# An explicit plan of pieces for both attentions of a two-layer hybrid model

## Chip, cores and metric

The kernel runs on one core of a Trainium2 chip, in one launch. The metric is the time of an execution on the device, in microseconds (us), as the median of several runs. Engines are named as in the profile: PE is TensorE's matmul, PEld its weight load, DVE is VectorE, ACT is ScalarE, POOL is GpSimd, SP is the engine that issues most of the DMAs.

## What is computed

One sequence of 512 tokens of width 1024 passes two layers in fp32. Layer 0 mixes two kinds of attention with 8 heads each, layer 1 has one kind with 16 heads; each is followed by a feed-forward network (FFN) with a short convolution. Cut to what matters here:

```python
# layer 0, first half: heads with a cumulated forget gate c
s = q_i @ k.T * scale + c_i - c_k            # causal
out = softmax(s) @ v
# layer 0, second half: an index picks 128 keys a query
score = sum_h iw * relu(iq_h @ ik.T)         # causal, 4 index heads
sel = top_k(score, 128)
logits = (q_lat @ c_kv[sel] + q_rope @ k_rope[sel]) * scale
out = softmax(logits) @ c_kv[sel]            # then w_uv
# layer 1: blocks of 256 keys, own block and chosen earlier ones (all of them at this length)
out = softmax(concat(s_sel, s_own)) @ v
x = x + out @ w_out;  x = x + ffn(rmsnorm(x))
```

## The kernel before

Activations lie transposed, 1024 features as 8 tiles of 128 x 512. Every fp32 product is made of three matmuls of high and low parts (`mm3`, L159 to L161), so each operand is split: ACT casts the high part, DVE or POOL subtracts the low part. Weights come in chunks of 128 x 1024 (512 KB): SP loads one into a `raw` tile (three of them, L147), ACT casts it (L148), and POOL (L152, in layer 0's attention) or DVE (L154, in layer 1) makes the low part.

An attention has eight pairs of heads. The pieces of a pair are these:

- `ks`, `qs`: a projection of 24 matmuls into one of three PSUM banks named `mm`; then a scaling or a rotary embedding; then `stack_k` or `stack_q`, which put high and low parts of a head one above the other. That takes six DMAs for a k and three for a q, issued by SP (`move`, L244): for a q, two fill `a`, and a third rewrites `l` once `a` has its copy.
- `vals`, every second pair: a `v_group` of 96 matmuls of 256 columns from two weight chunks. The pairs 4 to 7 of layer 0 make k and v from a latent tile in short products instead (`mm_dk` at L705 and on, `mm_dv`).
- `soft`, for a head: four blocks of scores (L268, L269; in the first half a decay term at L344 before them), each followed by a DVE instruction that adds the mask and takes the maximum (L348) and by an exponential on ACT (L349); POOL divides (L353). The result lies in one of two `prt` tiles.
- `mix`, for a head: ten transposes (L372), their split into high and low parts (L128, L129), and eight value matmuls into one bank `o` (L381, L382).

Layer 0 also has three index scores (`index_scores`, with ReLUs at L618 and, for blocks 2 and 3, a copy on ACT and an addition on POOL at L623), and a selection for each of three blocks of queries (`select`): 16 rounds of a maximum (L629) and a replacement (L630) on DVE. They must be done before the scores of pair 4. Four parts of the output projection of pairs 0 to 3 (`out_proj("oe0_")`, `out_proj("oo0_")`) need only those pairs.

The order of the text comes from `heads`. A work list holds the pieces with the pair that they are due for; before a pair all work due for it is emptied, after each softmax a share of the work due for the next pair is done, and the value products run one head behind:

```python
            for e in range(2):
                probs = soft(...)
                n = len([1 for w in work if w[0] <= p + 1])
                for _ in range((n + 1 - e) // (2 - e)):
                    work.pop(0)[1]()
                if prev is not None:
                    finish(prev)
                prev = (p, e, probs)
```

Written in the letters of the change (s a softmax, m a value product, k, q, v the projections, i an index score, x a selection, o a part of the output projection; the first digit is the pair), the old order of layer 0 is: v0 i1 k0 i2 q0 i3, s00 k1 s01 q1 m00, s10 v2 k2 m01 s11 q2 x1 m10, s20 k3 x2 (first half) m11 s21 q3 x2 (rest) m20, s30 k4 x3 (first half) q4 m21 s31 v4 x3 (rest) m30, s40 k5 m31 s41 q5 m40, s50 k6 q6 m41 s51 v6 m50, s60 k7 q7 m51 s61 o0 m60, s70 o1 o2 m61 s71 o3 m70, m71. Layer 1 has the same without i and x: v0 k0 q0, s00 k1 s01 q1 m00, s10 v2 k2 m01 s11 q2 m10, and so on. Its first v group holds the norm's scale in its middle (`moba_scale`: `rstd_main` and `rope_scaled`, L217).

The framework that builds the kernel does not keep this order on each engine: it places an instruction when it expects its inputs and buffers to be ready, and the text's order decides between those that are.

## Time and profile before

| | |
|---|---|
| median of 3 runs | 1262.97 us (1261.54 to 1265.60) |
| the profiled execution | 1261.51 us, of which the span of instructions 1259.7 us |
| busy in the span | PE 1220.4, PEld 1018.3, DVE 810.9, ACT 557.4, POOL 357.7 us |
| first attention | 57.4 (first index score) to 276.0 us (first FFN matmul) |
| second attention | 637.0 (first v group) to 886.0 us |
| mean granted clock of TensorE | 0.993 |

The page gives shares of the whole span. How TensorE stands in a stage is read from the stretches, and what it waits for from the waits: a row there names the instruction that waited, what released it, the total, the times and the longest. The end of a matmul is modelled in the profile, so a stretch that is full of matmuls counts as busy even where they follow each other a little more slowly.

### The profile page before, as it was taken

To read this page: it belongs to the slowest core of one execution; us is meant where nothing else is said; L and a number is where in the kernel's file an instruction comes from. 1 tells how busy PE (TensorE), PEld (TensorE's weight loads), DVE (VectorE), ACT (ScalarE), POOL (GpSimd) and SP (SyncE) were. 2 spreads that over 40 slices of the span, in tenths; PEclk is the share of its full clock that TensorE was granted. 3 is DMA by queue.
4 is the path that set the end of the run, shared out by engine and by line. 5 is a ranking of instruction groups with operands and counts; after the bars stand their busy time and mean duration, and the time that the engine had idled before them with its cause. 6 is when DMAs were issued, how large, how long until landed. Compare 5 with 4: busy or idle time off the path is not lost.

```text
span 1259.7 us, 16807 instructions
## 1 busy us (share of the span) xinstructions
PE 1220.4 (97%) x5996; PEld 1018.3 (81%) x5996; DVE 810.9 (64%) x1489; ACT 557.4 (44%) x969; POOL 357.7 (28%) x394
## 2 busy tenths in 40 slices
PE   6889999999999999999999999999999999999997
PEld 4768778778888888888887888888888888888887
DVE  7889988675654555544666778787655555444555
ACT  5564667653332333333445556555433333332334
POOL 3665557542111111111213223332222111111110
PEclk9989999999999999999999999999999999999999
DMA  5333444222333322323325434331233332333321
GB/s 194 101 92 111 128 99 128 63 80 89 101 100 100 98 90 93 96 93 100 103 96 142 113 100 123 105 109 67 84 93 108 100 100 92 94 100 101 96 88 67
DMA packets 57379, 127.24 MB, mean 101 GB/s; under 512 B 7584, under 2 KB 21024, under 8 KB 57296
## 3 DMA queue, kind: packets, MB, share of 16 engines
q1 hardware_dynamic: 56368, 124.81, 33.2%
q10 hardware_dynamic: 864, 1.17, 0.3%
q8 instruction: 47, 0.77, 0.2%
q14 instruction: 36, 0.29, 0.1%
q0 software_dynamic: 64, 0.20, 0.0%
HBM read 104.13 MB, written 2.10 MB: 84 GB/s over the span
## 4 chain that ended last, share of the span: by engine, by line
PE 79%; DVE 10%; issue 5%; ACT 3%; DMA 2%; POOL 1%; POOLq 0%; ACTq 0%; DVEq 0%; SPq 0%
PE mm_g L160 6%; PE mm_g L161 6%; PE mm_g L159 6%; PE mm_u L161 6%; PE mm_u L159 6%; PE mm_u L160 6%; PE mm_d L161 6%; PE mm_d L160 6%; PE mm_d L159 6%; DVE tmask L630 2%; DVE m L629 1%; DMA mq_l<-mq_h 1%; PE t_m L372 1%; PE o_m L381 1%; PE mm_mk L160 1%
## 5 line engine op out<-in xcount | busy, mean ns | idle before, releaser
L434 POOL TENSOR_TENSOR cv<-cv,gs 128x512 f32<-128x512 f32 x44 | 57.1, 1298 | 546.2 <-ACT gs L433 546.2
L159 PE MATMUL mm_d<-a_h,wh_d 128*128 128x512 f32 (+1 forms) x384 | 142.8, 372 | 0.0
L160 PE MATMUL mm_d<-a_l,wh_d 128*128 128x512 f32 (+1 forms) x384 | 142.6, 371 | 0.0
L161 PE MATMUL mm_d<-a_h,wl_d 128*128 128x512 f32 (+1 forms) x384 | 142.6, 371 | 0.0
L503 DVE TENSOR_TENSOR us<-mm_u,cv 128x512 f32<-128x512 f32 x44 | 30.4, 692 | 168.1 <-PE mm_u L161 132.7
L160 PE MATMUL mm_g<-xl,wh_g 128*128 128x512 f32 x352 | 137.2, 390 | 0.4 <-DVE xl L175 0.4
L159 PE MATMUL mm_u<-xh,wh_u 128*128 128x512 f32 x352 | 137.3, 390 | 0.0
L161 PE MATMUL mm_u<-xh,wl_u 128*128 128x512 f32 x352 | 137.0, 389 | 0.0
L160 PE MATMUL mm_u<-xl,wh_u 128*128 128x512 f32 x352 | 137.0, 389 | 0.0
L161 PE MATMUL mm_g<-xh,wl_g 128*128 128x512 f32 x352 | 137.0, 389 | 0.0
L159 PE MATMUL mm_g<-xh,wh_g 128*128 128x512 f32 x352 | 137.0, 389 | 0.0
L148 ACT CAST wh_g<-raw_g 128x1024 fp32r<-128x1024 f32 x44 | 46.3, 1052 | 143.1 <-PE mm_g L160 141.6
L500 DVE TENSOR_TENSOR gs<-mm_g,RB 128x512 f32<-128x512 f32 x44 | 30.4, 691 | 118.2 <-PE mm_g L161 115.7
L128 ACT CAST wh_d<-raw_d 128x1024 fp32r<-128x1024 f32 x45 | 47.4, 1054 | 123.7 <-PE mm_u L160 103.4
L160 PEld LDWEIGHTS mm_d<-a_l,wh_d 128*128 128x128 f32 x384 | 72.3, 188 | 12.5
L159 PEld LDWEIGHTS mm_d<-a_h,wh_d 128*128 128x128 f32 x384 | 72.3, 188 | 12.5
L161 PEld LDWEIGHTS mm_d<-a_h,wl_d 128*128 128x128 f32 x384 | 72.3, 188 | 12.4
L160 PEld LDWEIGHTS mm_g<-xl,wh_g 128*128 128x128 f32 x352 | 66.1, 188 | 14.8 <-DVE xl L175 1.1
L161 PEld LDWEIGHTS mm_u<-xh,wl_u 128*128 128x128 f32 x352 | 66.1, 188 | 13.8
L159 PEld LDWEIGHTS mm_g<-xh,wh_g 128*128 128x128 f32 x352 | 66.1, 188 | 13.7
L161 PEld LDWEIGHTS mm_g<-xh,wl_g 128*128 128x128 f32 x352 | 66.1, 188 | 13.7
L160 PEld LDWEIGHTS mm_u<-xl,wh_u 128*128 128x128 f32 x352 | 66.1, 188 | 13.6
(778 smaller groups left out, 3072.4 us busy)
## 6 DMA issues: line engine op xcount, KB each, us to landing
raw_g<-in_w SPq DMA_DIRECT2D x44, 512.0 KB, 3.5
raw_u<-in_w SPq DMA_DIRECT2D x44, 512.0 KB, 3.6
raw_d<-in_w SPq DMA_DIRECT2D x41, 256.0 KB, 2.9
raw_d<-in_w SPq DMA_DIRECT2D x29, 192.0 KB, 2.6
raw_d<-in_w SPq DMA_DIRECT2D x34, 128.0 KB, 2.4
raw_oe<-in_w SPq DMA_DIRECT2D x8, 512.0 KB, 4.0
raw_mv<-in_w SPq DMA_DIRECT2D x8, 512.0 KB, 3.5
raw_mk<-in_w SPq DMA_DIRECT2D x8, 512.0 KB, 4.0
```

Of the source, the lines that this page charges most:

```text
L128: A.copy(dst_h, src)
L148: A.copy(wh, raw)
L159: PE.matmul(out, ah, bh, start=first, stop=False)
L160: PE.matmul(out, ah, bl, start=False, stop=False)
L161: PE.matmul(out, al, bh, start=False, stop=last)
L372: PE.transpose(t[:, n * P:n * P + P], probs[i][:, j * P:j * P + P], ident)
L381: PE.matmul(o[:, o0:o0 + w], vj, ph[:, c0:c0 + w], start=j == 0, stop=False)
L434: G.tensor_tensor(cv, cv, gs, op=OP.mult)
L500: V.tensor_tensor(gs, og, RB, op=OP.mult)
L503: V.tensor_tensor(us, ou, cv, op=OP.mult)
L629: V.max(m8, sc)
L630: V.match_replace(sc, m8, sc, -3e38)
```

## The change

Two strings, PLAN0 and PLAN1, list the pieces of each attention in order. `attention` runs through a plan and `attend` binds the letters to functions; `heads`, the work lists and their due numbers are gone. Each piece stands once in its plan. The selections are cut into quarters of four rounds (x10 is the first quarter for block 1). In layer 1 the scale of the norm is taken by whichever projection comes first, after its matmuls, and only once. Buffer counts stay as they were.

```diff
--- before.py
+++ after.py
@@ -47,6 +47,18 @@
 
 N_BIG, N_V, N_TMP, N_COL, N_PR, N_W = 25, 2, 7, 8, 2, 3
 N_PSUM = {"mm": 3, "S": 2, "T": 2, "O": 1}
+
+
+
+PLAN0 = (
+    "v0 i1 i2 k0 q0 i3 k1 s00 s01 q1 v2 x10 s10 m00 k2 s11 x11 m01 x12 q2 x13 x20 m10 k3 m11 k4 x21 s20 "
+    "x22 x30 s21 q3 m20 s30 x31 x32 s31 q4 x23 v4 m21 m30 k5 x33 m31 s40 s41 q5 m40 k6 s50 q6 m41 s51 v6 "
+    "k7 m50 q7 s60 o0 m51 s61 m60 s70 o1 s71 m61 m70 o2 m71 o3 "
+)
+PLAN1 = (
+    "q1 q0 k0 k3 v0 s00 k1 q2 m00 k2 s01 s10 s11 q3 s20 q4 s21 m01 v2 m10 m11 k4 s30 s31 m20 m21 v4 k5 q6 "
+    "m30 q5 s40 m31 s41 m40 k6 s50 k7 s51 m41 v6 q7 o0 s60 s61 s70 m50 m51 s71 o1 m60 m61 o2 o3 m70 m71 "
+)
 
 
 def _pieces(c, bits):
@@ -524,34 +536,24 @@
                 done(2 * p + e, Q[1])
         last(Q[1])
 
-    def heads(pairs, work):
-
-
-        work = list(work)
-        prev = None
-
-        def finish(pr):
-            p, e, probs = pr
-            c = pairs[p]
-            mix(f"{c['nm']}{e}", e, probs, values[c["v"]], c["hv"] + e, c["y"])
-            if e == 1:
-                c["out"].append(halves(c["y"], f"o_{c['nm']}", c.get("lo", V)))
-
-        for p, c in enumerate(pairs):
-            while work and work[0][0] <= p:
-                work.pop(0)[1]()
-            c["y"] = tmp(f"y_{c['nm']}")
-            for e in range(2):
-                probs = soft(f"{c['nm']}{e}", e, c["q"], c["k"], c["bias"], c["decay"][e] if "decay" in c else None)
-                n = len([1 for w in work if w[0] <= p + 1])
-                for _ in range((n + 1 - e) // (2 - e)):
-                    work.pop(0)[1]()
-                if prev is not None:
-                    finish(prev)
-                prev = (p, e, probs)
-        finish(prev)
-        for w in work:
-            w[1]()
+    def attention(pairs, plan, pieces):
+
+
+        probs = {}
+        for step in plan.split():
+            kind, n = step[0], step[1:]
+            if kind == "s":
+                c, e = pairs[int(n[0])], int(n[1])
+                if e == 0:
+                    c["y"] = tmp(f"y_{c['nm']}")
+                probs[n] = soft(f"{c['nm']}{e}", e, c["q"], c["k"], c["bias"], c["decay"][e] if "decay" in c else None)
+            elif kind == "m":
+                c, e = pairs[int(n[0])], int(n[1])
+                mix(f"{c['nm']}{e}", e, probs.pop(n), values[c["v"]], c["hv"] + e, c["y"])
+                if e == 1:
+                    c["out"].append(halves(c["y"], f"o_{c['nm']}", c.get("lo", V)))
+            else:
+                pieces[kind](int(n))
 
     values = {}
 
@@ -676,7 +678,7 @@
 
         c = {"nm": f"f{p}", "v": ("f", p // 2), "hv": 2 * (p % 2), "bias": causal, "out": fo, "lo": G,
              "decay": [(selr[:, P + h:P + h + 1], ck) for h in (2 * p, 2 * p + 1)]}
-        return c, ([vals] if p % 2 == 0 else []) + [ks, qs]
+        return c, ks, qs, vals
 
     def dsa(p):
         def vals():
@@ -707,24 +709,16 @@
             c["k"] = stack_k(o, f"dk{p}")
 
         c = {"nm": f"d{p}", "v": ("d", p // 2), "hv": 2 * (p % 2), "bias": [causal[0]] + tmask[1:], "out": do}
-        return c, [ks, qs] + ([vals] if p % 2 == 0 else [])
-
-    pairs, work = [], []
-    for n in range(8):
-        c, w = (fox if n < 4 else dsa)(n % 4)
-        pairs.append(c)
-        if n == 0:
-            w = [x for i, f in enumerate(w) for x in (f, lambda i=i: index_scores(i + 1))]
-        elif n == 2:
-            w.append(lambda: select(1, range(16)))
-        elif n > 2 and n < 5:
-            w[1:1] = [lambda n=n: select(n - 1, range(8))]
-            w.append(lambda n=n: select(n - 1, range(8, 16)))
-        work += [(n, f) for f in w]
-        if n == 7:
-            work.append((7, lambda: out_proj("oe0_", fo, part=[0])))
-    work += [(8, lambda m=m: out_proj("oe0_", fo, part=[m])) for m in range(1, 4)]
-    heads(pairs, work)
+        return c, ks, qs, vals
+
+    def attend(made, plan, **pieces):
+        for k, n in (("k", 1), ("q", 2), ("v", 3)):
+            pieces[k] = lambda p, n=n: made[p][n]()
+        attention([m[0] for m in made], plan, pieces)
+
+    attend([fox(p) for p in range(4)] + [dsa(p) for p in range(4)], PLAN0,
+           i=index_scores, x=lambda n: select(n // 10, range(n % 10 * 4, n % 10 * 4 + 4)),
+           o=lambda m: out_proj("oe0_", fo, part=[m]))
     acc = sq_acc(1)
     out_proj("oe1_", do, lambda d: prep(d, 1, acc))
     lo_on_pool = False
@@ -739,33 +733,31 @@
 
 
     def moba_scale():
-        rstd_main(accs[2], "n2")
-        rope_scaled()
+
+        if 2 in accs:
+            rstd_main(accs.pop(2), "n2")
+            rope_scaled()
 
     mo = ([], [])
 
     def moba(p):
         def vals():
-            values["m", p // 2] = v_group(f"mv{p // 2}_", moba_scale if p == 0 else None)
+            values["m", p // 2] = v_group(f"mv{p // 2}_", moba_scale)
 
         def qs():
-            c["q"] = stack_q(rope(proj(f"mq{p}"), f"mq{p}"), f"mq{p}")
+            o = proj(f"mq{p}")
+            moba_scale()
+            c["q"] = stack_q(rope(o, f"mq{p}"), f"mq{p}")
 
         def ks():
-            c["k"] = stack_k(rope(proj(f"mk{p}"), f"mk{p}"), f"mk{p}")
+            o = proj(f"mk{p}")
+            moba_scale()
+            c["k"] = stack_k(rope(o, f"mk{p}"), f"mk{p}")
 
         c = {"nm": f"m{p}", "v": ("m", p // 2), "hv": 2 * (p % 2), "bias": causal, "out": mo[p // 4]}
-        return c, ([vals] if p % 2 == 0 else []) + [ks, qs]
-
-    pairs, work = [], []
-    for n in range(8):
-        c, w = moba(n)
-        pairs.append(c)
-        work += [(n, f) for f in w]
-        if n == 7:
-            work.append((7, lambda: out_proj("oo0_", mo[0], part=[0])))
-    work += [(8, lambda m=m: out_proj("oo0_", mo[0], part=[m])) for m in range(1, 4)]
-    heads(pairs, work)
+        return c, ks, qs, vals
+
+    attend([moba(p) for p in range(8)], PLAN1, o=lambda m: out_proj("oo0_", mo[0], part=[m]))
     accs[3] = sq_acc(3)
     out_proj("oo1_", mo[1], lambda d: prep(d, 3, accs[3]))
     fin = {}
```

## Rows read from the trace of the kernel before

**Rows 1.** The page, busy time and share of the span

```profile
PE 1220.4 (97%) x5996; PEld 1018.3 (81%) x5996; DVE 810.9 (64%) x1489; ACT 557.4 (44%) x969; POOL 357.7 (28%) x394
```

**Rows 2.** Stretches: PE, PEld, DVE, ACT, POOL busy (count), PE clock, DMA, GB/s

```profile
57.40:276.00 218.60, 208.91 (x1091) 171.78 (x1090) 180.19 (x455) 134.01 (x302) 132.57 (x174) 0.98 0.36 99
637.00:886.00 249.00, 243.01 (x1388) 208.07 (x1387) 188.34 (x400) 136.09 (x296) 70.17 (x86) 1.00 0.37 105
276.00:637.00 361.00, 360.46 (x1593) 297.85 (x1592) 196.32 (x250) 125.57 (x152) 67.29 (x51) 1.00 0.32 98
```

**Rows 3.** Waits of TensorE, 57.4 to 276 us: total, times, longest

```profile
PE s_f L268 <- DMA fq_a<-fq_l: 3.3, 1, 3.3
PE ix L268 <- ACT rl L618: 2.3, 1, 2.3
PE t_f L372 <- DVE pt_f_0l L129: 1.9, 4, 1.3
PE mm_dq L159 <- DVE dv L129: 1.8, 1, 1.8
```

**Rows 4.** Waits of TensorE, 637 to 886 us

```profile
PE s_m L268 <- DMA mq_l<-mq_h: 3.3, 3, 1.3
PE s_m L268 <- DMA mq_a<-mq_l: 1.0, 1, 1.0
```

**Rows 5.** Stretches at a granted clock of 0.50: PE busy, clock, DMA, GB/s

```profile
83.90:90.70 6.80, 6.13 (x19) 0.50 0.09 22
169.20:172.60 3.40, 3.40 (x9) 0.50 0.16 18
```

**Rows 6.** Timeline of TensorE at the ends of two waits

```profile
84.57 0.58 PE L268 MATMUL s_f<-fk_h,fq_a 128*128 128x256 f32 x1 [3.29 <-DMA fq_a<-fq_l]
...
168.65 0.50 PE L159 MATMUL mm_dq<-xh,wh_dq 128*128 128x512 f32 x1 [1.77 <-DVE dv L129]
```

**Rows 7.** Timeline of the SP queue, 79 to 85 us (start, length)

```profile
79.24 0.33 SPq L147 DMA_DIRECT2D raw_fq<-in_w  x1
...
80.14 0.59 SPq L244 DMA_DIRECT2D fq_a<-fq_l  x1
84.54 0.46 SPq L244 DMA_DIRECT2D fq_l<-fq_h  x1
```

**Rows 8.** Timeline of POOL, 67 to 79 us

```profile
67.61 2.84 POOL L152 TENSOR_TENSOR wl_fq<-raw_fq,wh_fq 128x256 fp32r<-128x256 f32 x4 [4.36 <-ACT wh_fq L148]
...
71.65 1.02 POOL L623 TENSOR_TENSOR tmask<-rl,cmask 128x384 f32<-128x384 f32 x1
72.75 3.21 POOL L623 TENSOR_TENSOR tmask<-rl,tmask 128x384 f32<-128x384 f32 x3
75.92 3.29 POOL L152 TENSOR_TENSOR wl_fv<-raw_fv,wh_fv 128x256 fp32r<-128x256 f32 x4
```

**Rows 9.** DMA issues: KB each, median us to landing

```profile
fq_a<-fq_l SPq DMA_DIRECT2D x1, 128.0 KB, 4.4
fq_l<-fq_h SPq DMA_DIRECT2D x1, 128.0 KB, 2.2
...
mq_l<-mq_h SPq DMA_DIRECT2D x1, 128.0 KB, 5.2
```

**Rows 10.** Selection instructions: durations min/median/max and starts; then groups of one width

```profile
L629 DVE MAX8 m<-tmask x48: 414/561/696, 67.1 to 168.5; 128x8 f32<-128x256 f32 x16, 128x8 f32<-128x384 f32 x16, 128x8 f32<-128x512 f32 x16
...
L629 DVE MAX8 m<-tmask 128x8 f32<-128x512 f32 x16 | 11.0, 685 | 0.2
L630 DVE MATCH_REPLACE8 tmask<-m,tmask 128x512 f32<-128x512 f32 x16 | 10.8, 676 | 0.0
```

**Rows 11.** Stretches of the first attention, columns as in rows 2

```profile
57.00:97.00 40.00, 34.38 (x148) 27.48 (x148) 33.75 (x94) 25.11 (x51) 28.55 (x34) 0.91 0.35 104
97.00:177.00 80.00, 76.25 (x437) 64.36 (x437) 73.63 (x191) 42.23 (x98) 41.85 (x59) 0.98 0.40 107
```

**Rows 12.** Timeline of VectorE, the scaled cosine of the second attention

```profile
648.84 0.69 DVE L217 TENSOR_TENSOR CR<-CT,RB 128x512 f32<-128x512 f32 x1 [1.22 <-ACT RB L211]
```

## Prediction

> **What bounds the kernel now.** I read the page's engine shares first, then the stretches by stage, then TensorE's waits in the two attentions, then its clock, then the rows round the longest waits.
>
> TensorE is busy for 1220.4 us of a span of 1259.7 [rows 1]. That leaves 39 us, and the change touches only part of them. The stretches [rows 2] set both attentions (57.4 to 276.0 us and 637.0 to 886.0 us) beside the FFN between them. In the FFN TensorE idles for 361.0 - 360.5 = 0.5 us. In the first attention it idles for 218.6 - 208.9 = 9.7 us, in the second for 249.0 - 243.0 = 6.0 us. The named waits there are few: in the first attention 3.3 us for a stack move of fq_a, 2.3 us for an index ReLU, 1.9 us for a low part of the transposed probabilities and 1.8 us for dv [rows 3]; in the second four waits for moves of mq, 4.3 us together [rows 4]. The clock comes on top: in two stretches of 6.8 and 3.4 us the granted clock is 0.50, which is 1.2 of 2.4 GHz [rows 5]. The first stretch begins at 83.9 us, inside the wait for fq_a, which ends at 84.57; the second at 169.2, just after the wait for dv ended at 168.65 [rows 6]. Before both falls TensorE stood idle (3.3 and 1.8 us); after the waits for mq, 1.3 us at most, the clock stays at 1.00 [rows 2]. Half a clock costs half of its busy time: 6.1/2 = 3.1 us and 3.4/2 = 1.7 us.
>
> So all that a new order can win is idle time plus clock: 9.7 + 6.0 + 3.1 + 1.7 = 20.5 us. The program computes the same work: both plans hold every piece once (8 k, 8 q, 4 v, 16 scores, 16 value products, 4 output parts, and in the first attention 3 index scores and 12 quarters of the selections).
>
> **Why the big wait happens.** The move of fq_a is issued at 80.14 us, directly behind a weight load (raw_fq) of 79.24, on the same SP queue [rows 7]. Before that the queue stood still. The load could go out only when its raw buffer was free, that is when POOL had finished the low part of an earlier weight tile (75.92 + 3.29 = 79.21 us [rows 8]). POOL was late because the four additions of index score 2 (1.02 + 3.21 us, from 71.65) came first, although it had idled for 4.36 us before 67.61 [rows 8]. Once issued, the move shared the DMA engines with 512 KB of weights: 4.4 us to landing, where the next move, with no load before it, took 2.2 [rows 9]. The moves of mq show the same: 5.2 us for mq_l [rows 9].
>
> **The change part by part.** First: the text's order is not the engines' order. The selection of block 1 stands behind q2 in the old text, but the first selection row runs at 67.1 us [rows 10], before the first score. The build places each piece as soon as its inputs and buffers are expected ready, and the text gives precedence only. The plan therefore shifts who wins a queue; it does not move whole pieces. Two heads' score rows remain bounded by the two prt buffers, which stay: a third softmax waits for a value product's transposes, whatever the plan says.
>
> *Start of the first attention* (v0 i1 i2 k0 q0 i3 k1 s00 in place of v0 i1 k0 i2 q0 i3 s00 k1). Index score 2 takes precedence over k0. Its ReLUs, its copies and its four POOL additions, 4.2 us, can then fall into POOL's idle 4.36 us. The weight tile's low part ends some 4 us earlier (near 75 us), so do the load and the moves behind it, and fq_a lands near 80.5 instead of 84.5, before TensorE's wait begins (84.57 - 3.29 = 81.3 [rows 6]). I take the wait and its half clock as gone: 3.3 + 3.1 = **6.4 us**. Bounds: 0 (POOL does not use the gap) to 6.4. I take the upper end because the gap found, 4.36, exceeds the 3.3 us that are missing.
>
> *The index wait (2.3 us)* hangs on ACT, which casts the cumulated gate first; index scores now come even earlier, so it stays: 0 (between +2.3 and -2.3, since index 2 may double it or k0 may fill it).
>
> *Selections in quarters.* Same instructions (48 maxima and 48 replacements). A quarter of block 3 is 4 x (685 + 676) ns = 5.4 us of VectorE [rows 10]. In 97 to 177 us VectorE is busy for 73.6 of 80 us [rows 11], so any quarter that wins precedence delays something: a low part of a value product or of dv. TensorE's cover is a projection, 24 matmuls of 361.0/1593 = 0.227 us [rows 2] = 5.4 us. One quarter is just covered, two in a row are not. I leave the waits for low parts and dv and their clock (1.9 + 1.8 + 1.7 = 5.4 us) where they are: net 0, bounds -5.4 to +10.5 (three places of 1.8 + 1.7 us, the places of the third rival).
>
> *Second attention* (q1 q0 k0 k3 v0 s00 in place of v0 k0 q0 s00 k1). Projections go ahead by one to three pairs, so a q's two moves into a (4.4 us behind a load) and the one back into l (5.2) must end under later work: 9.6 us. In the old order q of a pair was the last thing before its scores, with one projection (5.4 us) or less as cover. Now two projections or a v group (96 matmuls at half width, twice 5.4 = 10.9 us) mostly lie between. I take the four waits as gone: **4.3 us**; bounds 0 to 4.3.
>
> The norm's scale moves behind the first projection. It needs the transposes and the chain on VectorE to the scaled cosine at 648.84 us [rows 12], some 12 us after the stretch begins; q1, q0 and k0 hold three banks of mm, 3 x 5.4 = 16.3 us, so k3 finds q1's bank free again. Cost 0; without that cover TensorE would wait for each us that the chain is late. The guard in the scale function adds no instruction. The extra pieces ahead of q0 and k0 put three moves and a load of q1 on SP before theirs; v0's 10.9 us and k3's 5.4 us cover them.
>
> *Ends.* Value products two heads behind and o3 before or between the last ones: none of the waits of [rows 3, 4] lies at an end (they are for f, dq and mq pieces that come earlier), so 0, bounds -1 to +3.
>
> Here the page of the profile leaves room for doubt. By rows, TensorE's idle time in the second attention is 6.0 us, of which the moves are 4.3. The Trainium skill (Perfetto Trace Analysis, Identifying the Most-Contended Engine) says that headroom is to be judged by the weight loads' busy share, not by matmul busy time; that share is 208.1/249.0 = 84% in the second attention and 297.9/361.0 = 83% in the full FFN, so by the rule nothing is left there and the sum would be 6.4 alone, 1256.6 us. I keep the rows: shorter matmuls need more weight loads per us, and the waits are there by name.
>
> **Sum.** 6.4 + 4.3 = 10.7 us. The profiled execution took 1261.5 us (span 1259.7 and 1.8 around it), 1.5 under the median of 1262.97; taken off the median, 10.7 gives **1252 us**.
>
> **Rivals.**
>
> *1. The waits only change their names (1260 to 1265, say 1263).* Loads and moves keep one queue, and the sequence of weight loads hardly changes. For it: four waits of the same kind in the second attention come at irregular places, so they are where the build's expectation of a landing was too early, and it expects the same afterwards. Then 10.7 us go and come back. Against it: longer leads. The Trainium skill (DMA: Bandwidth & Descriptors, Queues, rings and completion order) says that each DMA engine consumes a queue's descriptors in ring order; the 4.4 against 2.2 us above agree, and by that rule a move behind a load stays slow under any plan.
>
> *2. Everything yields (1243).* All idle time and both half clocks go: 1263 - 20.5. For it: each wait is short, and a plan with pieces split finely has fill for each. Against it: the index wait and the selections are bound to ACT and VectorE.
>
> *3. Selections starve TensorE (1269).* The plan puts two quarters together at three places (x13 x20 before m10, x22 x30 before s21, x31 x32 before s31), just where k4 and q3 have been used up earlier. VectorE, already 92% busy [rows 11], then delays the low parts as it delayed dv: 1.8 + 1.7 us at each, 10.5 us in all. With the second attention's 4.3 us won and the first wait not, 1263 + 10.5 - 4.3 = 1269. It decides as soon as TensorE idles for more than the 9.4 us that it idles now between 57 and 177 us (5.6 + 3.8 [rows 11]) plus the 4.3 won later. Against it: the build runs selections early wherever VectorE is free, as it does now.
>
> **Chances.** The forecast 0.48, rival 2 0.12, rival 1 0.2, rival 3 0.2. A measurement of this kernel tells 0.3% (3.8 us) from no change. Faster: 0.48 + 0.12 = 0.6; same 0.2; slower 0.2. The range goes from rival 2 with the end's 1 us, 1242, to rival 3, 1269: it takes in rival 1 and the bounds of single terms, and leaves out about 2 in 10. The likeliest case alone spans 1247 to 1258 (5.4 us more won, or the first term lost).
>
> **What would show it.** Right: no wait of scores for fq_a near 81 us, POOL's additions of index 2 before 71 us, no half clock at 84 to 91 us, no wait for a mq move of over 0.3 us, TensorE's idle time in the second attention near 2 us. Wrong: a move's wait at other scores (rival 1); VectorE over 95% busy with a new half clock between 97 and 177 us (rival 3); a wait for the norm chain at the fourth projection of the second attention.

## The result and the profile after

The changed kernel takes 1245.68 us (median of 4 runs, 1245.14 to 1246.56), the kernel before, on the same chip, 1262.74 us (4 runs, 1261.54 to 1265.60). The ratio is 0.9859 with a 95% interval of [0.9842, 0.9877]: 17 us faster, where 10.7 us were forecast. The profiled execution took 1245.54 us with a span of 1243.8, so it shows 15.9 us less span than the profile of before.

The page, busy time and share of the span [rows 1]:

```profile
PE 1211.7 (97%) x5996; PEld 1012.4 (81%) x5996; DVE 812.3 (65%) x1489; ACT 556.2 (45%) x969; POOL 357.5 (29%) x394
```

The same instructions as before on every engine. TensorE is busy for 8.7 us less and its weight loads for 5.9 less; the other engines stay within 1.4 us. The stretches by stage, with the columns of [rows 2] (first attention, second attention, the FFN between them):

```profile
56.80:268.00 211.20, 203.78 (x1090) 168.34 (x1089) 180.80 (x456) 134.22 (x302) 131.99 (x174) 1.00 0.39 103
628.70:869.50 240.80, 240.12 (x1386) 206.83 (x1386) 189.34 (x400) 134.71 (x296) 70.53 (x86) 1.00 0.39 108
268.00:628.70 360.70, 360.55 (x1593) 297.82 (x1593) 195.94 (x250) 125.60 (x152) 67.18 (x51) 1.00 0.32 98
```

Against [rows 2] the first attention is 218.6 - 211.2 = 7.4 us shorter, the second 249.0 - 240.8 = 8.2 us; the FFN stays within 0.3 us, and what lies before and behind adds up to nothing (0.6 less ahead of the first attention, 0.6 more behind the second). In the first attention TensorE's busy time falls by 5.1 us and its idle time from 9.7 to 7.4 us. The granted clock there is 1.00 throughout: both half-clock stretches of [rows 5], 3.1 + 1.7 = 4.8 us by the prediction's working, are gone, and they are nearly all of the 5.1. In the second attention idle time falls from 6.0 to 0.7 us, and busy time by 2.9.

The runs agree on the clock's part: the four of the kernel after have a mean granted clock of 0.996 to 0.997, the profile of before 0.993, and the 14 to 20 runs of the kernel before beside each experiment 0.992 to 0.994 on average. Taken as lost time, (1 - clock) x 1255 us, that is an estimate, from above, of 4 to 6 of the 17 us.

TensorE's waits in the first attention, 56.8 to 268 us [rows 3]:

```profile
PE ix L280 <- ACT rl L620: 2.6, 2, 2.3
PE o_f L393 <- ACT pt_f_0h L140: 1.5, 1, 1.5
PE t_f L384 <- DVE pt_f_0l L141: 1.2, 1, 1.2
PE s_f L356 <- DVE mx_f L360: 1.0, 2, 0.7
PE s_f L280 <- DMA fq_a<-fq_l: 0.6, 1, 0.6
```

and all that is left of them in the second, 628.7 to 869.5 us [rows 4]:

```profile
PE bc_n L216 <- DVE y_n L213: 0.3, 1, 0.3
```

The wait for fq_a went from 3.3 to 0.6 us, the one for dv is gone (1.8), the one for low parts shrank by 0.7: 5.2 us in all. New are 1.5 us for a high part of the transposed probabilities and 1.0 us for the scores' maxima; with 0.3 more for the index ReLUs these take 2.8 back, and 5.2 - 2.8 = 2.4 is about the idle time won (9.7 - 7.4 = 2.3). All four waits for mq moves are gone.

Now the SP queue and POOL round the place of the old wait for fq_a. SP, 74 to 82 us [rows 7]:

```profile
74.94 0.33 SPq L159 DMA_DIRECT2D raw_fk<-in_w  x1
...
76.58 0.55 SPq L256 DMA_DIRECT2D fq_a<-fq_h  x1
77.18 0.60 SPq L256 DMA_DIRECT2D fq_a<-fq_l  x1
78.20 0.33 SPq L159 DMA_DIRECT2D raw_fq<-in_w  x1
81.60 0.46 SPq L256 DMA_DIRECT2D fq_l<-fq_h  x1
```

POOL, 66 to 79 us [rows 8]:

```profile
66.56 1.03 POOL L625 TENSOR_TENSOR tmask<-rl,cmask 128x384 f32<-128x384 f32 x1 [3.92 <-ACT rl L624]
67.66 3.21 POOL L625 TENSOR_TENSOR tmask<-rl,tmask 128x384 f32<-128x384 f32 x3
...
72.08 2.84 POOL L164 TENSOR_TENSOR wl_fq<-raw_fq,wh_fq 128x256 fp32r<-128x256 f32 x4
74.87 3.30 POOL L164 TENSOR_TENSOR wl_fv<-raw_fv,wh_fv 128x256 fp32r<-128x256 f32 x4
```

POOL's additions of index score 2 do come first now, as forecast, but they did not fill the gap: POOL idles for 3.92 us ahead of them, because ACT hands over the weighted ReLU that they add (L624) only at 66.56. They push wl_fq from 67.61 to 72.08, and wl_fv ends at 78.17, 1.0 us earlier than before and not 4. What did change is the queue: the two moves of fq_a now stand ahead of the load of raw_fq, not behind it, and go out at 76.58 and 77.18 while that load still waits for POOL (78.20, just behind 78.17). They land no faster: the third move, which waits for them, goes out at 81.60, 4.4 us behind the second, as before (80.14 to 84.54). Another load, raw_fk, stands 2.2 us ahead of that second move. What is won is the issue, 3.0 us earlier.

### The profile page after: what moved, and what is told of

Its sections match the earlier page's. It is cut to its first block, busy times and chain, and to the rows that moved or that the text cites. A ratio compares the mean times of both kernels' runs of the same rounds, so it can differ in the third digit from the quotient of the medians.

```text
span 1243.8 us, 16808 instructions
## 1 busy us (share of the span) xinstructions
PE 1211.7 (97%) x5996; PEld 1012.4 (81%) x5996; DVE 812.3 (65%) x1489; ACT 556.2 (45%) x969; POOL 357.5 (29%) x394
## 4 chain that ended last, share of the span: by engine, by line
PE 85%; DVE 8%; issue 4%; ACT 1%; DMA 1%; POOL 0%; POOLq 0%; ACTq 0%; DVEq 0%
PE mm_g L172 6%; PE mm_g L171 6%; PE mm_g L173 6%; PE mm_u L171 6%; PE mm_u L172 6%; PE mm_u L173 6%; PE mm_d L171 6%; PE mm_d L172 6%; PE mm_d L173 6%; PE t_m L384 1%; DVE tmask L632 1%; DVE m L631 1%; PE mm_mk L171 1%; PE mm_mq L173 1%; PE mm_mk L173 1%
## 5 line engine op out<-in xcount | busy, mean ns | idle before, releaser
L172 PEld LDWEIGHTS mm_d<-a_l,wh_d 128*128 128x128 f32 x384 | 72.3, 188 | 12.4
L173 PEld LDWEIGHTS mm_g<-xh,wl_g 128*128 128x128 f32 x352 | 66.1, 188 | 13.7
L171 PEld LDWEIGHTS mm_u<-xh,wh_u 128*128 128x128 f32 x352 | 66.1, 188 | 13.6
```

Of the source, the lines that this page charges most:

```text
L171: PE.matmul(out, ah, bh, start=first, stop=False)
L172: PE.matmul(out, ah, bl, start=False, stop=False)
L173: PE.matmul(out, al, bh, start=False, stop=last)
```

## The experiments

Twelve kernels, each against the kernel before on the same chip. The stage lengths are of the profiled execution, from the first matmul of a stage to the first of the next (by that count the kernel before has 248.6 in the second attention and the one after 240.7). "fq_a" and "mq" are TensorE's waits for those moves.

| kernel | median us | ratio, 95% interval | first att. | second att. | fq_a | mq |
|---|---|---|---|---|---|---|
| before | 1262.7 | | 218.6 | 248.6 | 3.3 | 4.3 |
| after | 1245.7 | 0.9859 [0.9842, 0.9877] | 211.3 | 240.7 | 0.6 | 0 |
| e1 plan 0 only | 1256.4 | 0.9960 [0.9945, 0.9975] | 212.8 | 249.2 | 0.9 | 2.9 |
| e2 plan 1 only | 1254.0 | 0.9940 [0.9922, 0.9957] | 218.8 | 240.7 | 3.6 | 0 |
| e3 i2 ahead | 1269.7 | 1.0059 [1.0041, 1.0078] | 229.8 | 250.0 | 2.3 | 1.4 |
| e5 k1 ahead | 1270.4 | 1.0072 [1.0039, 1.0106] | 225.7 | 253.1 | 3.2 | 4.4 |
| e9 i2 and k1 ahead | 1267.7 | 1.0051 [1.0031, 1.0072] | 223.7 | 250.3 | 2.0 | 2.6 |
| e12 old start, new rest | 1258.3 | 0.9971 [0.9957, 0.9985] | 216.4 | 250.9 | 3.9 | 2.0 |
| e4 moves ahead of loads | 1257.9 | 0.9962 [0.9950, 0.9975] | 217.7 | 244.5 | 0.9 | 0.2 |
| e6 selections whole | 1246.3 | 0.9892 [0.9864, 0.9920] | 211.8 | 240.4 | 0.7 | 0 |
| e7 value products later | 1264.3 | 1.0023 [1.0004, 1.0041] | 219.7 | 252.0 | 3.6 | 2.8 |
| e8 projections earlier | 1263.8 | 1.0014 [0.9996, 1.0032] | 216.7 | 250.1 | 3.9 | 0 |
| e10 both of these | 1270.5 | 1.0075 [1.0051, 1.0098] | 217.9 | 256.5 | 3.3 | 0 |
| e11 index score 1 earlier | 1253.0 | 0.9936 [0.9911, 0.9962] | 228.5 | 240.4 | 0 | 0 |

In e11 the first attention begins 9 us earlier, since its first index score does. In e2, e7, e8 and e10 the first attention's order is that of before: five profiles of one order lie between 216.7 and 219.7 us, with 3.4 to 13.7 us of half clock in them, so a difference of 3 us between two single profiles there says little. The second attention is told apart better: all six profiles with its old order lie at 248.6 to 253.1 us (before, e1, e3, e5, e9, e12), all four with the plan at 240.4 to 240.7 (after, e2, e6, e11). Within the old order the waits for mq vary from 1.4 to 4.4 us and the stage gets no shorter where they are small: in the other five, waits of 1.5 to 2.6 us for POOL's division of prt stand beside them. A named wait is therefore not a price by itself.

**The two plans, one at a time.** OLD0 and OLD1 are the old orders written as plans, letter by letter.

```diff
e1:  -PLAN1 = (the plan)   +PLAN1 = OLD1
e2:  -PLAN0 = (the plan)   +PLAN0 = OLD0
```

> The new plan in the first attention, the old order written as a plan in the second. My theory (each attention lost its own waits: 7.3 us of the span in the first, 7.9 us in the second, and the two have nothing to do with each other): 1262.7 - 7.9 = 1255, first attention about 211 us long as in the changed kernel, second about 249 us as before. Rival (the gain is shared, as when work leaves one attention for the other, or half of it is an accident of the clock at the start): under 3 us or over 12 us faster than before.

> The old order in the first attention, the new plan in the second. My theory: 1262.7 - 7.9 = 1255, the first attention with the wait for fq_a and both half clocks as before (218 us), the second 241 us with no wait for a mq move. Rival (gain not separable): the two single plans together do not add up to the 17 us of both, by over 4 us.

Each plan gains alone, and in its own stage: the first attention of e1 is 5.8 us shorter than before and its second as long, the second of e2 is 7.9 us shorter and its first as long. By the ratios the two gain 0.40% and 0.60%, together 1.0% of 1.41%. By the stages of the profiles they add up: 5.8 + 7.9 = 13.7 of the 15.2 us (7.3 + 7.9) of the whole, and the 1.5 missing are a half clock of 3.4 us at 64.5 us in e1, behind the wait for the index ReLU, which the profile of the kernel after doesn't have. Part of what the runs' times lack beyond that is clock: the mean granted clock is 0.994 in e1, 0.993 in e2 and 0.997 in the kernel after, against 0.993 in the runs before beside e1 and e2. As time, an estimate, the two single plans win 0.14% by the clock together and the whole plan 0.39%; the 0.16% left over is within the intervals.

**Selections whole.**

```diff
-PLAN0 = "... v2 x10 s10 m00 k2 s11 x11 m01 x12 q2 x13 x20 m10 k3 m11 k4 x21 s20 x22 x30 s21 q3 ..."
+PLAN0 = "... v2 s10 m00 k2 s11 m01 q2 x10 x11 x12 x13 m10 k3 x20 x21 m11 k4 s20 s21 q3 x22 x23 ..."
```

> The changed kernel with the quarters of the selections put together where the old order had them (all of block 1 after q2, halves of blocks 2 and 3), the rest of both plans as changed. As predicted (quarters net 0, the build fills VectorE's free time with selections wherever they stand): 1245 to 1248, no wait for dv. Rival (the quarters are what removed the wait for dv, 1.8 us, and its half clock, 1.7): 1249 to 1252, with the wait for dv or for a low part back near 160 to 170 us.

1246.3 against 1245.7 us, on two chips; the ratios' intervals overlap (0.9892 and 0.9859), and both attentions are within 0.5 us of the kernel after. Cutting the selections into quarters is worth nothing that can be told, and the wait for dv stayed away without it.

**The start of the first attention.** Four starts, the second attention in its old order in all of them.

```diff
 before: v0 i1 k0 i2 q0 i3 s00 k1 s01 q1 ... (old rest)
 e3:     v0 i1 i2 k0 q0 i3 s00 k1 s01 q1 ... (old rest)
 e5:     v0 i1 k0 i2 q0 i3 k1 s00 s01 q1 ... (old rest)
 e9:     v0 i1 i2 k0 q0 i3 k1 s00 s01 q1 ... (old rest)
 e12:    v0 i1 k0 i2 q0 i3 s00 k1 s01 q1 ... (the plan's rest)
```

> The old order of both attentions with one swap: index score 2 ahead of k0. Theory A (as predicted: POOL's additions of index 2 move into its idle time, and with them the load and the moves behind it): the wait for fq_a falls from 3.3 us to under 1 us, the half clock at 84 us goes, about 1256 to 1257, and the low part of the weight tile ends some 4 us earlier than 79.2 us. Theory B (what counts is that the moves stand ahead of the weight load on SP, in the order that the build makes of it): the same time, but the low part ends within 1.5 us of 79.2 us and the load of raw_fq is issued after the two moves into fq_a. Rival (k1 and not the index score is what covers the wait): no change, 1262 to 1263.

> The old order of both attentions with one swap at the start: k1 before the first softmax, index scores as of old. Theory C (after the swap of the index score alone left 2.3 us of the wait for fq_a: the wait goes only when both swaps are made, one that puts the moves ahead of the load and one that gives TensorE k1 to do meanwhile): the wait for fq_a stays over 1.5 us, 1260 to 1264. Rival (k1 alone covers it): the wait is under 1 us and the half clock at 84 us is gone, 1256 to 1258.

> The old orders of both attentions, but with the whole new start: index score 2 ahead of k0 and k1 ahead of s00 (v0 i1 i2 k0 q0 i3 k1 s00 s01 q1, then as before). On SP the two moves of fq_a now come ahead of the load of raw_fq, and k1's projection lies between q0's and the scores. Theory (both swaps are needed and together suffice): the 3.3 us wait for fq_a falls to 1 us or less and the half clock of 6.8 us at 84 us goes, so the first 100 us are some 5 us shorter; the four waits for mq moves in the second attention stay near 4 us; the kernel would be at 1256 to 1258 us. Rival (a change of the start alone is paid back later in the first attention, as it was by each swap alone, by waits for dq_a, dv and dk moves with half clocks): the wait is gone, yet the kernel is at 1262 us or more, and the gain of the full plan in the first attention is then one of its later order too. Second rival (the wait for fq_a needs more than the start): a wait of over 2 us for fq_a stays.

> The fourth corner of a square for the first attention, the second attention in its old order in all four: old start with old rest is the kernel before, new start with old rest ran at 1267.7, new start with new rest at 1256.4; this is the old start (v0 i1 k0 i2 q0 i3 s00 k1 s01 q1) with the plan's rest. Theory (the start's order decides the wait for fq_a alone, the rest decides whether the waits for dq_a and dv come up): the wait for fq_a is back at 3.3 us with its 6.8 us of half clock at 84 us; no wait for dq_a over 0.5 us, none for dv over 1 us; the first attention is 212.8 + 5.8, some 217 to 219 us, and the kernel at 1258 to 1262 us, so the start is worth 3 to 6 us when the rest is new, where it cost 6 us when the rest was old. Rival (start and rest fit only together): waits for dq_a or dv of 2 us or more come up here as they did with the new start and the old rest, and the kernel is at 1264 us or more. Second rival (the start is worth nothing, the rest wins all): the kernel is within 1.5 us of 1256.4.

All three changes of the start alone make the kernel slower, against the theories of e3 and e9. On SP, e3 and e9 have the moves of fq_a ahead of raw_fq, e5 has them behind it as before, so index score 2 is what turns them round; POOL ends wl_fv at 80.52 us in e3, later than the 79.21 of [rows 8], so POOL's idle time is not how. Counted from the first index score, the second move lands after 27.1 us in the kernel before and 27.0 in e5, after 26.1, 25.9 and 24.8 us in e3, e9 and the kernel after (the first two with a half clock of 3.4 us at 64 to 65 us that the other three lack). The turn alone leaves 2.3 us of the wait in e3; with k1 as well, 0.8 us are left at this place in e9 (the 2.0 of the table are two waits). TensorE's waits in the first attention of e9:

```profile
PE s_d L273 <- DMA dq_a<-dq_l: 4.2, 2, 2.7
PE mm_dq L164 <- DVE dv L134: 3.2, 2, 2.9
...
PE s_f L273 <- DMA fq_a<-fq_l: 2.0, 2, 1.2
```

POOL and SP of e9, 167 to 173 us:

```profile
167.89 3.01 POOL L157 TENSOR_TENSOR wl_dq<-raw_dq,wh_dq 128x256 fp32r<-128x256 f32 x4
...
170.92 0.33 SPq L152 DMA_DIRECT2D raw_oe<-in_w  x1
...
171.36 0.46 SPq L249 DMA_DIRECT2D dq_a<-dq_h  x1
...
171.88 0.59 SPq L249 DMA_DIRECT2D dq_a<-dq_l  x1
```

A load stands still until POOL frees a raw buffer (167.89 + 3.01 = 170.90), the moves of dq_a go out right behind it and take 4.2 us, and TensorE waits for 2.7 us, to 176.20. But the kernel before has the same meeting at the same place, without a wait. Its SP queue, its move's landing in the window 170 to 177 us, and TensorE:

```profile
171.07 0.33 SPq L147 DMA_DIRECT2D raw_oe<-in_w  x1
...
172.02 0.59 SPq L244 DMA_DIRECT2D dq_a<-dq_l  x1
```

```profile
dq_a<-dq_l SPq DMA_DIRECT2D x1, 128.0 KB, 4.4
```

```profile
177.05 0.36 PE L268 MATMUL s_d<-dk_h,dq_a 128*128 128x256 f32 x1
```

There the move lands at 176.42, and TensorE, held up by the wait for dv and its half clock, comes for it only at 177.05. In e9 it comes at 173.49 and waits: what the start has won is mostly waited away here, since the load and the moves are hardly earlier. Counted from the first index score, e9 still begins these scores 1.9 us ahead of the kernel before, and from there to the end of the stage it takes 7.0 us longer. The rows of that stretch hold the second wait for dq_a (1.5 us; here the meeting is new, the move goes out at 192.80 behind a load of 191.85 and takes 4.2 us, where the one of before took 2.2), a wait for dv (2.9), a half clock at 205.4 us (1.5, half of TensorE's busy time in it) and two waits for high parts (0.7): 6.5 us together. With the plan's rest (e12) neither the waits for dq_a nor those for dv come up: of over 0.5 us the first attention of e12 has only these,

```profile
PE s_f L273 <- DMA fq_a<-fq_l: 3.9, 1, 3.9
PE ix L273 <- ACT rl L613: 2.3, 1, 2.3
PE o_f L386 <- ACT pt_f_0h L133: 1.4, 1, 1.4
PE t_f L377 <- DVE pt_f_0l L134: 1.2, 1, 1.2
```

and its clock is at 0.50 for 6.8 us from 83.9 us, as before. The four corners of the square, as ratios to before:

| | old rest | new rest |
|---|---|---|
| old start | 1 | 0.9971 [0.9957, 0.9985] |
| new start | 1.0051 [1.0031, 1.0072] (e9) | 0.9960 [0.9945, 0.9975] (e1) |

With the old rest the new start costs 0.5% (6 us). With the new rest the first attention is 216.4 - 212.8 = 3.6 us shorter in e1 than in e12, by one profile each, of which the half clock at 84 us in e12 makes up 2.4 (half of the 4.8 us that TensorE is busy in it). In the runs' times the difference is 1 to 2 us with intervals that overlap, so that the new start gains at all is not shown by the times. Start and rest don't add up: the rest's worth is 0.3% behind the old start and 0.9% behind the new.

**Moves ahead of loads.** In the order of before, the load of a pair's k and q weights is queued on SP only behind the last move of the q two pairs earlier. No piece of the text moves.

```diff
-        nc.sync.dma_start(raw, w_d[idx[name]])
...
+        p = int(p) + 4 * (m[0] == "d") - 2 if p else -1
+        with tc.issue_after(qmoves[m[0] == "m", p]) if (m[:1] == "m", p) in qmoves else nullcontext():
+            nc.sync.dma_start(raw, w_d[idx[name]])
...
-        move(l[LO], h[HI])
+        ins = move(l[LO], h[HI])
+        if nm[1] == "q":
+            qmoves[nm[0] == "m", int(nm[2]) + 4 * (nm[0] == "d")] = ins.ins
```

> The kernel before, with its own order, where the weight loads of a pair's k and q are queued on SP behind the last move of the q two pairs earlier; nothing else is told to the build. My theory (the waits are moves behind loads on one queue): the waits for fq_a and mq moves go, with the half clock at 84 us, 10.7 us in all: 1252, unless loads now come late, which would show as waits of projections for weight casts. Rival (the lead of the projections in the plan is what counts, the queue is not): the waits stay, 1260 to 1265.

The waits for mq fall from 4.3 to 0.2 us, and the second attention is 4.1 us shorter, well below the 248.6 to 253.1 of the other profiles with the old order. So the place of the moves behind loads is enough to make these waits; nothing else of the old order has to change. The moves also land sooner, the last one in 2.2 us at the median instead of 3.8:

```profile
mq_a<-mq_l SPq DMA_DIRECT2D x8, 128.0 KB, 2.2
mq_l<-mq_h SPq DMA_DIRECT2D x8, 128.0 KB, 2.2
```

TensorE's waits there:

```profile
PE o_m L389 <- ACT pt_m_0h L129: 0.8, 4, 0.3
PE t_m L380 <- POOL prt_m L361: 0.6, 2, 0.3
PE bc_n L210 <- DVE y_n L207: 0.5, 1, 0.5
PE s_m L276 <- DMA mq_a<-mq_l: 0.2, 1, 0.2
```

In the first attention the wait for fq_a falls to 0.5 us at its old place (0.9 with another pair's) and the half clock at 84 us is gone as well, but the wait for dv and its half clock stay, and other waits come in, for a late weight tile of dq (1.65 us, with a half clock right behind it) and for a high part (1.34 us). There the gain is 0.9 us, and the kernel is at 1257.9 us, not at the 1252 of the theory.

**What of the second plan does it.** The value products one softmax later (e7), the projections one pair earlier (e8), both and the output parts kept for the end (e10); the first attention in its old order.

```diff
 before: v0 k0 q0 s00 k1 s01 q1 m00 s10 v2 k2 m01 s11 q2 m10 s20 k3 m11 ...
 e7:     v0 k0 q0 s00 k1 s01 q1 s10 m00 v2 k2 s11 m01 q2 s20 m10 k3 s21 ...
 e8:     v0 k0 q0 k1 q1 s00 v2 k2 s01 q2 m00 s10 k3 m01 s11 q3 m10 s20 ...
 e10:    v0 k0 q0 k1 q1 s00 v2 k2 s01 q2 s10 m00 k3 s11 m01 q3 s20 m10 ...
         ... s60 m50 o0 s61 m51 o1 s70 m60 s71 o2 m61 o3 m70 m71
```

> The old order of both attentions, but in the second the value products stand one softmax later (two heads behind), projections where they were. My theory (the second attention gained by the projections' lead, which hides the moves): the waits for mq moves stay at 3 us or more, second attention 247 to 250 us, 1260 to 1263. Rival (the lag of the value products is what gains): under 244 us, 1255 to 1258.

> The old order of both attentions, but in the second every projection stands one pair earlier, value products one head behind as of old. My theory: the waits for mq moves fall under 1 us, second attention 243 to 245 us (the moves' 4.3 us and no more), 1257 to 1259. Rival (the particular order of the new plan is needed): over 246 us, waits of scores or value products elsewhere.

> The old order of the first attention; in the second the projections one pair earlier, the value products one softmax later, and the output parts kept for the last four value products (s60 m50 o0 s61 m51 o1 s70 m60 s71 o2 m61 o3 m70 m71). Theory (the lead takes the move waits away, the later value products and the kept output parts cover the end): the second attention is 241 to 244 us long, no mq move wait over 0.3 us, no wait of over 1 us at its end, and the kernel is at 1255 to 1257 us. Rival (the particular order of the plan is needed): a wait of over 1 us or a half clock appears somewhere in the second attention, which is 246 us or longer, and the kernel is at 1259 us or more.

Later value products alone gain nothing. The lead alone takes the waits for mq away, and yet the stage is no shorter: at its end TensorE waits 2.0 us for the last head's split,

```profile
PE mm_oo__0_8196 L164 <- ACT o_m_h L133: 2.0, 1, 2.0
```

and a half clock of 3.4 us begins as the wait ends (867.3 us). With both it is 7.9 us longer than before. TensorE's waits in the second attention of e10:

```profile
PE mm_oo__0_8196 L164 <- ACT o_m_h L133: 4.3, 3, 2.0
PE t_m L377 <- DVE pt_m_0l L134: 1.9, 3, 1.3
PE s_m L273 <- DVE mx_m L353: 0.8, 2, 0.4
```

The output projection waits for the last heads, and the clock is at 0.50 for 3.4 us twice, at 864.9 and 875.1 us, behind the two longer ones of these waits (1.9 us to 863.86, 2.0 us to 874.96). The plan ends without any such wait. So a lead is enough against the moves, and the end of the stage needs an order of its own, which my two did not have; which letters of the plan's end give it was not tried further.

**The index wait.** In the kernel after, index score 1 is written ahead of the gate's scan.

```diff
+    index_scores(1)
     R = slice(96, 128)
...
-    "v0 i1 i2 k0 q0 i3 k1 ..."
+    "v0 i2 k0 q0 i3 k1 ..."
```

> The kernel after, with index score 1 traced ahead of the gate's scan rather than behind v0. ACT's ReLUs of index score 1 then come ahead of its casts of the gate and of the scaling of v0. Theory (the 2.3 us that TensorE waits for an index ReLU is the gate's casts standing ahead of the ReLUs on ACT): that wait is below 0.5 us, and the kernel is 2 us faster than the kernel after, 1243 to 1244.5 us. Rival (the wait changes its name, since the scores of index 1 come before v0's matmuls have given ACT time): the wait for a ReLU or for a PSUM bank stays at 2 us or comes back as a wait of v0 or k0, and the kernel stays within 1.5 us of 1245.7 or is slower.

7 us slower than the kernel after (0.8% by the ratios to before). The wait for an index ReLU went on to the next index score and grew. ACT of e11, 68 to 72 us:

```profile
68.16 0.61 ACT L660 CAST ck<-lu 32x512 fp32r<-32x512 f32 x1 [2.08 <-DVE lu L658]
68.80 1.24 ACT L664 CAST ck<-lu 32x512 fp32r<-32x512 f32 x2
70.06 0.87 ACT L620 ACTIVATE rl<-ix 128x384 f32<-128x384 f32 x2
```

ACT stands for 2.08 us at the cast of the gate, which waits for DVE's scan, and the ReLUs behind it come late: TensorE waits 3.6 us (to 70.60), and inside that wait, at 68.9 us, a half clock of 6.8 us begins. Another of 3.4 us begins at 48.4, right behind a wait of 1.2 us for iq_a, and later come waits for dq_a (1.6 us) and fq_l (1.3 us). In the kernel after, the same casts stand ahead of index score 1's ReLUs (from 60.32 us, 1.93 idle before them). By these rows the 2.3 us are the gate's casts, since whichever index score comes behind them waits; no run took the casts away, so that is read and not shown. Moving one index score doesn't help.

## Why the prediction was right, and where not

**The sign and the size.** Faster was right; 10.7 us were forecast and 17 measured (15.9 by the profiles). 1245.7 us lies in the range of 1242 to 1269, just below the 1247 to 1258 of the likeliest case. By its number the second rival (everything yields, 1243 us) came nearest, by its mechanism it did not come: of the 20.5 us of idle time and clock, 2.3 + 5.3 + 4.8 = 12.4 were won, and TensorE still idles for 7.4 us in the first attention. The other 3.5 of the 15.9 are busy time (2.9 in the second attention, 0.3 in the first, 0.3 in the FFN), which neither the forecast nor that rival had. So the direction and the named waits were foreseen, and a good part of the size was not.

**Start of the first attention, 6.4 us.** The rows that it named went: 2.7 of the 3.3 us wait and the half clock at 84 us (3.1), 5.8 us together by the profile. As the worth of the start this is not shown: alone it costs 6 us (e9), and with the new rest it is worth 3.6 us by two profiles and 1 to 2 by the runs. The half clock, too, is not tied to the wait in every execution: e8, with the first attention's order of before and a wait of 3.26 us to 83.84, has none there,

```profile
83.90:90.70 6.80, 6.80 (x36) 5.87 (x37) 6.18 (x25) 5.63 (x17) 4.04 (x7) 1.00 0.16 27
```

while the seven other profiles with a wait of 2.2 us or more for fq_a do have one. The step that failed is the mechanism: "index score 2's additions can then fall into POOL's idle 4.36 us", wl_fv near 75 us. POOL's gap is not to be had, since the additions wait for ACT's weighted ReLUs; wl_fv ended 1.0 us earlier here, and 1.3 later in e3. The moves turned round on the SP queue instead: ahead of a load that waits for POOL, no longer behind it. The prediction had read that queue correctly ("the load could go out only when its raw buffer was free") and then sought the remedy at POOL, when the nearer one was the order of the two on SP. The sign that the prediction named for it, the additions of index 2 before 71 us, came true and showed nothing; the end of wl_fv was the one to look at. The step also looked no further than the wait itself: e3, e5 and e9 show that with the old rest TensorE then waits for dq_a and dv, and the kernel gets slower by 0.5 to 0.7%.

**The index wait stays.** It did (2.6 us), and the rows agree with the reason given; e11, which was to test it, only moved the wait to the next index score.

**Quarters of selections, net 0.** Right within what e6 can tell. But the 5.4 us that the same step left where they are (low parts, dv and its half clock) were won nearly whole: 0.7 + 1.8 + 1.7 = 4.2 us, within the bound of -5.4. The step had put dv down to VectorE being full of selections. VectorE is fuller after, 67.82 us busy of the 71 from 97 to 168 us,

```profile
97.00:168.00 71.00, 68.31 (x389) 57.55 (x388) 67.82 (x177) 39.75 (x94) 38.18 (x53) 1.00 0.41 111
```

which is 95.5%, the sign given for the third rival, and no half clock follows. The wait for dv had another cause, which rows of before show. VectorE, 164 to 169 us:

```profile
164.83 0.68 DVE L630 MATCH_REPLACE8 tmask<-m,tmask 128x512 f32<-128x512 f32 x1
166.80 1.19 DVE L228 TENSOR_TENSOR ry_dq<-ry_dq,rs_dq 128x512 f32<-128x512 f32 x1 [1.30 <-POOL rs_dq L227]
167.92 0.68 DVE L129 TENSOR_TENSOR dv<-mm_dv,dv 128x512 fp32r<-128x512 f32 x1
```

and after:

```profile
162.20 0.67 DVE L141 TENSOR_TENSOR dv<-mm_dv,dv 128x512 fp32r<-128x512 f32 x1
...
162.88 0.65 DVE L240 TENSOR_TENSOR ry_dq<-ry_dq,rs_dq 128x512 f32<-128x512 f32 x1
```

Before, VectorE stood idle for 1.30 us at the rotary addition (ry_dq), which waited for a product from POOL, with dv's low parts queued behind it. After, both of dv's low parts (157.93 and 162.20 us) come ahead of the addition. In e9 a later addition of the same kind waits for 2.65 us, with dv behind it and a wait of 2.9 for TensorE. That the order of these two is the cause is read from the rows; no run changed it alone.

**The second attention, 4.3 us.** All four waits went, as forecast, and by the mechanism given: e4, which only takes the moves from behind the loads, gains 4.1. In the plan the lead does it, and not faster moves: as a whole mq's moves land no sooner after. Their medians are

```profile
mq_a<-mq_h SPq DMA_DIRECT2D x8, 128.0 KB, 3.5
mq_a<-mq_l SPq DMA_DIRECT2D x8, 128.0 KB, 3.2
mq_l<-mq_h SPq DMA_DIRECT2D x8, 128.0 KB, 2.6
```

against 2.2, 2.2 and 3.8 before. Counted move by move, 16 of the 24 go out while a weight load of SP is under way, with a median of 3.9 us to landing, the other 8 with 2.2; before it was 12 and 12, with 4.2 and 2.2. The ring order cited with the first rival (the Trainium skill, DMA: Bandwidth & Descriptors, Queues, rings and completion order) agrees with these counts. Whether order in a ring or the sharing of the DMA engines makes a move behind a load slow, no run tells. The rival built on it falls all the same, since nobody waits for these moves any more.

The term was too small by 3.9 us: 1.0 us of short waits by name (5.3 of idle time gone, not 4.3), and 2.9 us of busy time. The clock is 1.00 in both, the instructions are the same, and the ends of matmuls are modelled, so I read the 2.9 us as matmuls that followed each other more slowly before. It belongs to the order and not to one execution: from the stage's first matmul to the next stage's, TensorE is busy for 239.7 to 240.0 us in all four profiles with the plan, for 242.6 and 242.8 in before and e1, and for 242.1 in e4, where the waits for mq are gone as well. From start to start of the matmuls, 1.5 us of it lie in the value products and 1.3 in the v groups. No row of the waits names what for, and no run singled it out: the cause of these 2.9 us is open. "All that a new order can win is idle time plus clock" is the step that failed here. The rule that the prediction weighed against its rows (the Trainium skill, Perfetto Trace Analysis, Identifying the Most-Contended Engine) names the weight loads' busy share, beside the rate of arithmetic, as the measure of headroom. That 84% leaves nothing to win was the prediction's reading of it, by the FFN's 83%. 8.2 us were won, at 206.83/240.8 = 86% after, so 84% was not this stage's limit.

**Norm chain and ends, 0.** The scale's wait is 0.3 us (0.6 before), and the end has no wait: right for this plan. e8 and e10 show that the end's bound of +3 us was too small for plans like it: theirs cost 2.0 and 4.3 us of waits and one or two half clocks.

**The third rival** (selections starve TensorE, 1269) did not come. That e3, e5 and e9 stand at 1268 to 1270 us is a coincidence: their waits are for dq_a and dv, not for selections.

## What to carry to other kernels

Where small moves and large loads share an issuing queue, look first at what each move stands behind: a load that waits for its buffer holds every move behind it, and the move then lands late as well (4.2 to 4.4 us here, 2.2 without a load ahead). Putting the moves ahead, or giving them one more projection of lead, took away nearly every wait of this kind in the second attention. A gain at one place is only a gain once the rest of the stage has been read again: a change of order at the start, right by its own rows, brought TensorE too early to a meeting of load and moves that had stood 90 us further down all along, hidden by other waits, and new waits behind it made the kernel slower. Before a late landing is called new, look for the same rows in the kernel before.

## What the runs showed of the hardware

A short wait costs more than its length when the clock falls with it, and whether it falls varies between executions. The same wait of 2.33 us for the index ReLU is met by 3.4 us of granted clock 0.50, which begins within 0.4 us of the wait's end, in the profiles of e1, e2, e3, e7, e9 and e12, and by none in those of before, after, e4, e5, e6, e8 and e10. The stretch from 63.4 to 66.8 us in the kernel after and in e12, where the wait ends at 63.40 and at 63.78:

```profile
63.40:66.80 3.40, 3.40 (x18) 2.83 (x19) 3.05 (x7) 2.59 (x7) 0.24 (x1) 1.00 0.55 154
63.40:66.80 3.40, 3.02 (x9) 2.64 (x10) 3.05 (x7) 1.36 (x5) 0.00 (x0) 0.51 0.45 154
```

The spread of the runs goes with it: 17 runs of the kernel before beside e12 lie from 1257.85 us (clock 0.997) to 1266.26 us (0.990), the four of the kernel after, whose profile has no half clock between its start and 1236 us, within 1.4 us at 0.996 to 0.997. So a wait taken away is worth its length, and beside it up to half of 3.4 or 6.8 us in some of the executions, and one profile alone can't price it.
